# GpSimd's two-operand work in the mixers goes to VectorE, its scalings to ScalarE, and two expert splits move behind the selection

## The chip, the core and the metric

The kernel runs on one core of a Trainium2 chip. The core has five instruction queues that run side by side, each in the order in which its instructions stand: TensorE for matrix products (PE, with its weight loads as PEld), VectorE (DVE), ScalarE (ACT), GpSimd (POOL) and SyncE (SP), which issues the transfers. They wait for each other by semaphores. The metric is the time of one execution on the device in microseconds (us).

## The reference

Two layers over 256 latent tokens and 256 context tokens, 1024 channels wide. Each layer is a mixer of three branches and then a channel mixer: a dense SwiGLU in layer 0, and eight experts, of which each token takes two, in layer 1.

```python
def token_mixer(h, hc, ...):                 # one layer's mixer, cut
    zp, zr, zq, zk, zv, zg = jnp.split(h @ w_in, splits, axis=-1)      # 1024 -> 5,344
    ...                                                                # context tokens alike
    wkv, wkv_c = bidirectional_wkv(lat, cx, need_ctx_out)              # a recurrence, both ways
    nat = neighbourhood_attention(q, k, ...)
    branches = (pool_branch(zp, pool_w, pool_scale),                   # mean over a window - identity
                rwkv_readout(wkv, lat, bonus_rk, gn_g, gn_b, gate_g2), nat)
    y = gated_merge(branches, zg, w_branch, w_out)                     # sum of sigmoid(gate) * proj

# the recurrence, for each head a 64 x 64 state S:
#   S = S * w_t - (S kk_t) kka_t^T + v_t k_t^T ;  o_t = S r_t
# the last part: out = sum over experts e of gate[e] * swiglu(h, w1[e], w3[e], w2[e])
```

## The kernel before

Everything is float32. A product is made of three: each operand is split into a rounded part `hi` and the rest `lo`, and TensorE adds hi·hi, hi·lo and lo·hi (lines L491 to L493, L246 to L248 and L1845 to L1847 are these three for different places). A weight tile of 128x1024 comes in by a transfer (`wraw`), ScalarE rounds it (`whi`, L204) and a second engine subtracts (`wlo`, L208, in `split`). Which engine does that, `wload` counts: in the mixers every other tile and the first two are GpSimd's, the rest VectorE's. In the dense layer every other tile is GpSimd's too, and in the experts none.

A mixer has these stages, and TensorE's order in them is written by lanes with fixed costs (class `Order`), so that products of the input projection fill the time in which a chain of the recurrence waits:

- the front (85 to 265 us in mixer 0, 1200 to 1320 us in mixer 1): the input projection tile by tile, a shift between tokens (`s`, L523, L525 and L527 take the product out of PSUM), and for each of four channel groups and two directions the recurrence's operands (`operands`, L630 to L651) and the pooled branch (`z`, L1206 to L1210);
- the attention, with the triangular solve of the recurrence beside it (`solve`, L791 to L832), to 436 us and 1490 us;
- the core (436 to 655 us and 1490 to 1610 us): eight rounds n over chunks of 64 tokens, both directions d in each round. `reads` multiplies the state's rows with `Ga` (L928) and copies `Y` out (L931); `products` makes the next chunk's matrices, for chunks that need an output in the `sm` banks (L871; L882 and L877 take them out), else in `ch` banks (L891, L882); `solved` (L939, L942) and `state` (L951, L960, L962) end the round. There are two `sm` banks, so the second direction's L871 begins when the first's L882 and L877 have emptied them;
- readout, merge and output projection.

In the core the other half of `Ga` comes from memory. `chunk` sends for it and scales it, for two heads of each direction:

```python
            for hh, p, q in self.HEADS:
                a = e["Ga"][q, hh]
                nc.sync.dma_start(a, src[p, :, 64:128])
                nc.gpsimd.tensor_tensor(a, a, g[q].to_broadcast([64, 4, 64]), op=OP.mult)
```

The transfer (L861) can start when L928 has read the `Ga` before it. The order of VectorE's instructions is made by a scheduler from the program; it is not written out.

Of the kernel before, what the change touches and what calls it, by code (L numbers as in the profile page):

```python
# [103 lines left out]
class Builder:  # L104
    def __init__(self, ctx, tc, I, out, dbg=None):
        self.ctx, self.tc, self.nc, self.I, self.out = ctx, tc, tc.nc, I, out
        self.dbg = dbg or {}
        self.nlo, self.lo_first = 0, 0
        self.pre, self.ahead = [], []
        self.raws, self.parted, self.pin = (), (), False  # L110
        self.nraw = self.nparts = 0
        self.banks = {}
        self.norm_banks = ExitStack()
        self.sq = self.rs = None
        self.hw = 512
        self.cpool = ctx.enter_context(tc.tile_pool(name="consts", bufs=1))
        self.dram = ctx.enter_context(tc.tile_pool(name="dr", bufs=1, space=DRAM))
        nc = self.nc
        cst = self.cpool.tile([128, C_N], F32, name="cst")
        nc.sync.dma_start(cst, I["cst"])  # L120
        self.cst = cst
        self.ident = cst[:, C_ID:C_ID + 128]
        self.mask = cst[:, C_MSK:C_MSK + 128]
        self.i2 = cst[:, C_I2:C_I2 + 64]
        self.ob = cst[:, C_OB:C_OB + 128]
        self.ones = cst[:, C_ON:C_ON + 128]
        self.tiny = ctx.enter_context(tc.tile_pool(name="tiny", bufs=6))
        hb = self.cpool.tile([40, 4, 128], F32R, name="hb")
        with tc.tile_pool(name="hb0", bufs=1) as hp:
            hb0 = hp.tile([40, 4, 128], F32, name="hb0")  # L130
            nc.sync.dma_start(hb0, I["heads"])
            nc.vector.tensor_copy(hb, hb0)
        self.hb = hb
        self.vec = []
        for l in range(2):
            v = self.cpool.tile([128, V_N], F32, name=f"vec{l}")
            nc.sync.dma_start(v, I["vec"][l])
            self.vec.append(v)
        self.mod = [[None] * 6 for _ in range(2)]
# [61 lines left out]
    def split(self, hi, lo, src, hi_eng="act", lo_eng="dve"):  # L201
        nc = self.nc
        if hi_eng == "act":
            nc.scalar.copy(hi, src)  # L204
        else:
            nc.vector.tensor_copy(hi, src)
        e = nc.gpsimd if lo_eng == "pool" else nc.vector
        e.tensor_tensor(lo, src, hi.bitcast(F32), op=OP.subtract)  # L208

    def wload(self, src, n, lo_eng=None, hi_eng="act"):  # L210
# [20 lines left out]
        for s, raw in raws:  # L231
            self.split(hi[:, s], lo[:, s], raw[:, :s.stop - s.start], hi_eng, lo_eng)
# [318 lines left out]
    def rwkv_front(self, l, full, order):  # L551
# [20 lines left out]
        self.split(lwh, lwl, lw, "act", "pool")  # L572
# [27 lines left out]
        def glo_tile():  # L600
            glo = yield from self.shifted_out(l, 1, T_GLO, full, self.u)
            nc.scalar.activation(glo[0:96, :], glo[0:96, :], AF.Tanh, scale=0.5)
            nc.gpsimd.tensor_scalar(glo[0:96, :], glo[0:96, :], 0.5, 0.5, op0=OP.mult, op1=OP.add)
            self.glo = glo
# [17 lines left out]
        def operands(c, d):  # L622
# [25 lines left out]
            nc.gpsimd.tensor_copy(st[:, :, 1, 0].rearrange("p (s n) -> p s n", s=2), o4(kk)[:, :, :, 0])  # L648
            nc.scalar.copy(s4(4), o4(vc))
            nc.gpsimd.tensor_tensor(s4(0), n4(G), o4(rc), op=OP.mult)  # L650
            nc.gpsimd.tensor_tensor(self.order(kd, 0), self.order(kd, 0), self.order(rc, d), op=OP.mult)  # L651
# [94 lines left out]
    def out_gates(self, l, n, order):  # L746
# [4 lines left out]
        for c in range(4):  # L751
# [6 lines left out]
            nc.scalar.copy(gate, gp)  # L758
            nc.gpsimd.tensor_scalar(bo, bo, v[:, V_GNB + c:V_GNB + c + 1], None, op0=OP.add)
            nc.gpsimd.tensor_tensor(bo, bo, gate, op=OP.mult)  # L760
            nc.sync.dma_start(self.bonus[c], bo)
            nc.gpsimd.tensor_scalar(gate, gate, v[:, V_GNG + c:V_GNG + c + 1], None, op0=OP.mult)
# [76 lines left out]
    def chunk(self, d, n, need_o):  # L839
# [17 lines left out]
        if n:  # L857
            g = self.gq[d][:, :, n - 1].unsqueeze(2)
            for hh, p, q in self.HEADS:
                a = e["Ga"][q, hh]  # L860
                nc.sync.dma_start(a, src[p, :, 64:128])  # L861
                nc.gpsimd.tensor_tensor(a, a, g[q].to_broadcast([64, 4, 64]), op=OP.mult)
# [82 lines left out]
    def state(self, e, new, d, n):  # L945
# [15 lines left out]
        for hh, p, q in self.HEADS:  # L961
            nc.gpsimd.tensor_tensor(nS[q], new["XV"][q, hh], g[q].to_broadcast([64, 4, 64]), op=OP.mult)  # L962
# [72 lines left out]
    def readout(self, l, n, pool):  # L1035
# [13 lines left out]
        for c in range(4):  # L1049
# [4 lines left out]
            nc.gpsimd.tensor_tensor(ga[c], ga[c], w, op=OP.mult)  # L1054
# [127 lines left out]
    def pool_branch(self, l, full, order):  # L1182
# [6 lines left out]
        def pool_tile(g):  # L1189
# [10 lines left out]
            for i, z in enumerate(zs):  # L1200
# [3 lines left out]
                while w < win:  # L1204
                    nxt = self.pb.tile([128, 272], F32, name="z", tag="z")
                    nc.gpsimd.tensor_tensor(nxt[:, :m - w], cur[:, :m - w], cur[:, w:m], op=OP.add)  # L1206
                    cur, m, w = nxt, m - w, 2 * w
                ti = t[:, 256 * i:256 * i + 256]
                nc.gpsimd.tensor_tensor(ti, cur[:, 8 - h:264 - h], iv, op=OP.mult)
                nc.gpsimd.tensor_tensor(ti, ti, z[:, 8:264], op=OP.subtract)  # L1210
# [12 lines left out]
    def branch_split(self, tiles, n, mixed=False):  # L1223
        res = []
        for t in tiles:
            hi = self.u2(n, F32R)
            lo = self.u2(n, F32R)
            self.split(hi, lo, t, "act", "dve" if mixed and len(res) % 2 == 0 else "pool")
# [3 lines left out]
    def merge_branch(self, l, b, br, f, full, gate, acc):  # L1232
# [10 lines left out]
        nc.gpsimd.tensor_tensor(acc, acc, gate, op=OP.add)  # L1243
# [10 lines left out]
    def merge_steps(self, l, b, br, f, full, gate, acc):  # L1254
# [9 lines left out]
        if acc is not None:  # L1264
            nc.gpsimd.tensor_tensor(acc, acc, gate, op=OP.add)

    def mixer(self, l, x, full, xnew, done=lambda: None):
# [13 lines left out]
        self.lo_mod, self.lo_pool, self.lo_first = 2, 1, 2  # L1281
# [116 lines left out]
        def early_gate(f):  # L1398
            g = lambda n: self.gp.tile([128, n], F32, name="gp", tag="gp")
            self.gate[f] = yield from self.gate_steps(l, 1, f, full, g, "pool")  # L1400
# [77 lines left out]
        br = self.branch_split(self.wkv, n, True)  # L1478
# [176 lines left out]
    def moe(self, l, x):  # L1655
        nc, tc, I = self.nc, self.tc, self.I
        ident = self.ident
        with ExitStack() as ex:
# [21 lines left out]
            with P2("scrm2", 3) as self.sp, tc.high_priority(100000):  # L1680
# [41 lines left out]
                sel = self.selected(0, pos, msk, two, keep)  # L1722
# [404 lines left out]
```

## Time and profile before

| | |
|---|---|
| device time, median of 3 runs | 2495.73 us (2491.53 to 2501.99) |
| the profiled execution | 2494.59 us |
| its span in the trace | 2492.8 us, 40223 instructions |
| its mean granted TensorE clock | 0.961 |
| busy in the span: PE, DVE | 2318.3 us (93%), 1809.5 us (73%) |
| busy in the span: ACT, POOL | 1276.6 us (51%), 576.6 us (23%) |

Times of the trace count from the start of the span. The profiled execution's own time is 1.8 us above its span, and 1.1 us below the median of the runs. The granted clock is a share of full speed: 0.50 in a stretch means 1.2 instead of 2.4 GHz.

### The profile page before, as it was taken

The page shows a single profiled execution, that of the slowest core. Times are in us where ns is not written, and L with a number is a line of the kernel's source. Part 1 is how long each engine was busy: PE and PEld are TensorE (multiplying, and loading weights), DVE is VectorE, ACT ScalarE, POOL GpSimd, SP SyncE. Part 2 cuts the span into 40 slices and gives each one's busy share as a digit, 9 for nine tenths or more (in the row PEclk, how much of TensorE's full clock was granted, in tenths as well). Part 3 has the DMA queues.
Part 4 walks back from the last instruction along what each step waited for, and adds up shares of the span by engine and source line. Part 5 has one row for each costly group of instructions (what it writes and reads, how often), then busy time and mean ns, then how long its engine had stood idle before and what let it go on. Part 6 is the DMA issues. An engine that isn't in the chain of part 4 may idle for free. (4 is left out here: it accounts for less than half of the span.)

```text
span 2492.8 us, 40223 instructions
## 1 busy us (share of the span) xinstructions
PE 2318.3 (93%) x15206; PEld 1858.1 (75%) x15206; DVE 1809.5 (73%) x2723; ACT 1276.6 (51%) x1864; POOL 576.6 (23%) x487
## 2 busy tenths in 40 slices
PE   6899999988899999999779889979999999999998
PEld 4567667777678888777566678768888888888876
DVE  3784667656677656875785755568999999989997
ACT  3553554222243222234554444347777777777775
POOL 1255421243351221122553335430000000000000
PEclk8999998999899999999989989989999999999999
DMA  6364233554433444772473326675999999999995
GB/s 250 95 168 132 77 98 93 173 151 154 144 118 104 150 144 144 235 241 78 128 186 97 116 89 198 194 262 177 367 351 339 360 363 336 343 361 344 356 343 194
DMA packets 224141, 514.33 MB, mean 206 GB/s; under 512 B 70490, under 2 KB 104666, under 8 KB 222786
## 3 DMA queue, kind: packets, MB, share of 16 engines
q1 hardware_dynamic: 223938, 511.67, 61.1%
q8 instruction: 122, 2.00, 0.3%
q14 instruction: 81, 0.66, 0.1%
HBM read 484.79 MB, written 26.74 MB: 205 GB/s over the span
## 5 line engine op out<-in xcount | busy, mean ns | idle before, releaser
L204 ACT CAST whi<-wraw 128x1024 fp32r<-128x1024 f32 (+2 forms) x753 | 754.3, 1019 | 615.9 <-DMA wraw<-in_ffn 178.9
L208 DVE TENSOR_TENSOR wlo<-wraw,whi 128x1024 fp32r<-128x1024 f32 (+2 forms) x629 | 756.4, 1232 | 137.3 <-ACT whi L204 126.5
L208 POOL TENSOR_TENSOR wlo<-wraw,whi 128x1024 fp32r<-128x1024 f32 (+2 forms) x124 | 263.9, 2129 | 722.3 <-ACT whi L204 714.6
L491 PE MATMUL mm<-h,whi 128*128 128x512 f32 (+1 forms) x864 | 347.7, 402 | 33.3 <-DVE s L527 13.6
L493 PE MATMUL mm<-h,wlo 128*128 128x512 f32 (+1 forms) x864 | 321.4, 372 | 11.9 <-DVE wlo L208 6.2
L492 PE MATMUL mm<-h,whi 128*128 128x512 f32 (+1 forms) x864 | 322.0, 373 | 5.5 <-DVE h L476 5.4
L1845 PE MATMUL mm<-whi,xh 128*128 128x512 f32 (+1 forms) x768 | 289.2, 377 | 0.0
L1846 PE MATMUL mm<-whi,xl 128*128 128x512 f32 (+1 forms) x768 | 288.1, 375 | 0.0
L1847 PE MATMUL mm<-wlo,xh 128*128 128x512 f32 (+1 forms) x768 | 281.5, 376 | 1.3 <-DVE wlo L208 1.3
L491 PEld LDWEIGHTS mm<-h,whi 128*128 128x128 f32 x864 | 172.4, 200 | 86.2 <-issue 36.1
L493 PEld LDWEIGHTS mm<-h,wlo 128*128 128x128 f32 x864 | 172.2, 199 | 42.7 <-DVE wlo L208 8.5
L492 PEld LDWEIGHTS mm<-h,whi 128*128 128x128 f32 x864 | 172.9, 200 | 33.5 <-DVE h L476 9.2
L247 PE MATMUL mm<-h,whi 128*128 128x512 f32 (+1 forms) x448 | 170.6, 382 | 2.6 <-DVE h L208 2.6
L248 PE MATMUL mm<-h,wlo 128*128 128x512 f32 (+1 forms) x448 | 170.8, 382 | 0.4 <-POOL wlo L208 0.3
L246 PE MATMUL mm<-h,whi 128*128 128x512 f32 (+1 forms) x448 | 169.8, 380 | 0.0
L1847 PEld LDWEIGHTS mm<-wlo,xh 128*128 128x128 f32 x768 | 144.1, 188 | 29.2 <-DVE wlo L208 2.1
L1846 PEld LDWEIGHTS mm<-whi,xl 128*128 128x128 f32 x768 | 144.4, 188 | 27.0
L1845 PEld LDWEIGHTS mm<-whi,xh 128*128 128x128 f32 x768 | 144.6, 188 | 26.5
L1874 PE MATMUL mm<-wlo,hh 128*128 128x512 f32 x352 | 139.6, 397 | 0.8 <-DVE wlo L208 0.8
L1873 PE MATMUL mm<-whi,hl 128*128 128x512 f32 x352 | 139.1, 395 | 0.0
L1872 PE MATMUL mm<-whi,hh 128*128 128x512 f32 x352 | 138.7, 394 | 0.0
L368 DVE SCALAR_TENSOR_TENSOR scr<-wraw,cb 128x512 f32<-128x512 f32 x96 | 75.7, 806 | 57.6 <-DMA wraw<-in_w_mod 57.0
(378 smaller groups left out, 4024.4 us busy)
## 6 DMA issues: line engine op xcount, KB each, us to landing
wraw<-in_moe SPq DMA_DIRECT2D x516, 512.0 KB, 5.5
wraw<-in_w_in SPq DMA_DIRECT2D x108, 512.0 KB, 3.7
wraw<-in_w_mod SPq DMA_DIRECT2D x96, 512.0 KB, 4.6
wraw<-in_ffn SPq DMA_DIRECT2D x60, 512.0 KB, 3.9
rakbv<-std SPq DMA_DIRECT2D x32, 640.0 KB, 5.3
wraw<-in_w_branch SPq DMA_DIRECT2D x48, 256.0 KB, 2.7
std<-st SPq DMA_DIRECT2D x16, 640.0 KB, 5.0
wraw<-in_w_out SPq DMA_DIRECT2D x13, 512.0 KB, 4.1
```

The source lines that it names most:

```text
L204: nc.scalar.copy(hi, src)
L208: e.tensor_tensor(lo, src, hi.bitcast(F32), op=OP.subtract)
L246: nc.tensor.matmul(ps, wh, xh, start=i == 0, stop=False)
L247: nc.tensor.matmul(ps, wh, xl, start=False, stop=False)
L248: nc.tensor.matmul(ps, wl, xh, start=False, stop=i == n - 1)
L491: nc.tensor.matmul(ps, wh, xh, start=i == 0, stop=False)
L492: nc.tensor.matmul(ps, wh, xl, start=False, stop=False)
L493: nc.tensor.matmul(ps, wl, xh, start=False, stop=i == n - 1)
L1845: nc.tensor.matmul(ps, xh[:, k0 + k], hi[:, w], start=k0 + k == 0, stop=False)
L1846: nc.tensor.matmul(ps, xl[:, k0 + k], hi[:, w], start=False, stop=False)
L1847: nc.tensor.matmul(ps, xh[:, k0 + k], lo[:, w], start=False, stop=k0 + k == 7)
L1874: nc.tensor.matmul(y, hid[k][0], lo[:, w], start=False, stop=k == KF - 1)
```

## The change

In the two mixers GpSimd keeps its memsets and nothing else. The splits of weights, of the branches and of the small `lw`, the products and sums of the operands (L650, L651), of the pooled branch (L1206, L1209, L1210), of `Ga` and `S` (L862, L962), of the readout (L1054) and of the merges (L1243, L1265) are VectorE's; two scalings and a small copy (L603, L762, L648) are ScalarE's, and two steps of the gate (L759, L760) become one VectorE instruction that reads PSUM. The dense layer's splits stay as they were. In the experts, the splits of the third and fourth weight tile get an ordering edge behind the selection matrices `sel` of the routing. VectorE's queue grows from 3297 to 3656 instructions, ScalarE's from 2493 to 2511, and GpSimd's falls from 496 to 103.

```diff
@@ split, wload
-        e.tensor_tensor(lo, src, hi.bitcast(F32), op=OP.subtract)
+        return e.tensor_tensor(lo, src, hi.bitcast(F32), op=OP.subtract)
...
-            self.split(hi[:, s], lo[:, s], raw[:, :s.stop - s.start], hi_eng, lo_eng)
+            ins = self.split(hi[:, s], lo[:, s], raw[:, :s.stop - s.start], hi_eng, lo_eng)
+            if self.nlo in self.late_lo:
+                self.behind(ins)
@@ front
-        self.split(lwh, lwl, lw, "act", "pool")
+        self.split(lwh, lwl, lw, "act", "dve")
-            nc.gpsimd.tensor_scalar(glo[0:96, :], glo[0:96, :], 0.5, 0.5, op0=OP.mult, op1=OP.add)
+            nc.scalar.activation(glo[0:96, :], glo[0:96, :], AF.Identity, scale=0.5, bias=half[0:96])
-            nc.gpsimd.tensor_copy(st[:, :, 1, 0].rearrange("p (s n) -> p s n", s=2), o4(kk)[:, :, :, 0])
+            nc.scalar.copy(st[:, :, 1, 0].rearrange("p (s n) -> p s n", s=2), o4(kk)[:, :, :, 0])
-            nc.gpsimd.tensor_tensor(s4(0), n4(G), o4(rc), op=OP.mult)
-            nc.gpsimd.tensor_tensor(self.order(kd, 0), self.order(kd, 0), self.order(rc, d), op=OP.mult)
+            nc.vector.tensor_tensor(s4(0), n4(G), o4(rc), op=OP.mult)
+            nc.vector.tensor_tensor(self.order(kd, 0), self.order(kd, 0), self.order(rc, d), op=OP.mult)
@@ gate of the readout
-            nc.scalar.copy(gate, gp)
-            nc.gpsimd.tensor_scalar(bo, bo, v[:, V_GNB + c:V_GNB + c + 1], None, op0=OP.add)
-            nc.gpsimd.tensor_tensor(bo, bo, gate, op=OP.mult)
+            nc.vector.scalar_tensor_tensor(bo, bo, v[:, V_GNB + c:V_GNB + c + 1], gp, op0=OP.add, op1=OP.mult)
-            nc.gpsimd.tensor_scalar(gate, gate, v[:, V_GNG + c:V_GNG + c + 1], None, op0=OP.mult)
+            nc.scalar.activation(gate, gp, AF.Copy, scale=v[:, V_GNG + c:V_GNG + c + 1])
@@ chunk, state, readout
-                nc.gpsimd.tensor_tensor(a, a, g[q].to_broadcast([64, 4, 64]), op=OP.mult)
+                nc.vector.tensor_tensor(a, a, g[q].to_broadcast([64, 4, 64]), op=OP.mult)
-            nc.gpsimd.tensor_tensor(nS[q], new["XV"][q, hh], g[q].to_broadcast([64, 4, 64]), op=OP.mult)
+            nc.vector.tensor_tensor(nS[q], new["XV"][q, hh], g[q].to_broadcast([64, 4, 64]), op=OP.mult)
-            nc.gpsimd.tensor_tensor(ga[c], ga[c], w, op=OP.mult)
+            nc.vector.tensor_tensor(ga[c], ga[c], w, op=OP.mult)
@@ pooled branch (three lines alike), merges (two alike), branch_split
-                    nc.gpsimd.tensor_tensor(nxt[:, :m - w], cur[:, :m - w], cur[:, w:m], op=OP.add)
+                    nc.vector.tensor_tensor(nxt[:, :m - w], cur[:, :m - w], cur[:, w:m], op=OP.add)
-            nc.gpsimd.tensor_tensor(acc, acc, gate, op=OP.add)
+            nc.vector.tensor_tensor(acc, acc, gate, op=OP.add)
-            self.split(hi, lo, t, "act", "dve" if mixed and len(res) % 2 == 0 else "pool")
+            self.split(hi, lo, t, "act", "dve")
@@ mixer, moe
-        self.lo_mod, self.lo_pool, self.lo_first = 2, 1, 2
+        self.lo_mod, self.lo_pool, self.lo_first = 2, 0, 0
-                sel = self.selected(0, pos, msk, two, keep)
+                sel = self.selected(0, pos, msk, two, lambda ins: setattr(self, "mark", keep(ins)))
+
+                self.late_lo = (3, 4)
```

The changed program's lines stand one to three further down than here; the rows below show each program's own. First VectorE's queue in the core of mixer 1, in the fifth of the eight rounds (it begins at 1561.8 us in the trace of before). `Y`, `Ga` and `Gr` are the copies and matrices named above, `gq` holds the scalings of one direction. Before:

```order
L931 COPY Y<-ch 128x256 x2
L882 TENSOR_TENSOR Ga<-sm,cst 64x256
L877 TENSOR_TENSOR Gr<-sm,cst 128x256
L882 TENSOR_TENSOR Ga<-sm,cst 64x256
L877 TENSOR_TENSOR Gr<-sm,cst 128x256
L942 COPY XV<-ch 64x256
```

and of the change:

```order
L932 COPY Y<-ch 128x256 x2
L863 TENSOR_TENSOR Ga<-Ga,gq_13337 64x256 x2
L863 TENSOR_TENSOR Ga<-Ga,gq_13338 64x256
L883 TENSOR_TENSOR Ga<-sm,cst 64x256
L878 TENSOR_TENSOR Gr<-sm,cst 128x256
L883 TENSOR_TENSOR Ga<-sm,cst 64x256
L878 TENSOR_TENSOR Gr<-sm,cst 128x256
L863 TENSOR_TENSOR Ga<-Ga,gq_13338 64x256
L943 COPY XV<-ch 64x256
L209 TENSOR_TENSOR wlo<-wraw,whi 128x1024
```

The scalings of `Ga`, which wait for their transfers, stand ahead of the instructions that empty the `sm` banks. Second, VectorE's queue in the front of mixer 0 (at 172 to 179 us in the trace of before), up to the instruction that takes a product of the projection out of PSUM. Before:

```order
L638 TENSOR_TENSOR s_1372<-s_1372,kz 128x512
L663 TENSOR_TENSOR V_687<-ch,cst 128x512
L643 TENSOR_TENSOR st<-s_1372,s_1367 128x8x64
L644 SCALAR_TENSOR_TENSOR s_1367<-s_1364,s_1367 128x512
L525 SCALAR_TENSOR_TENSOR s_1428<-mm,vec_73,s_1428 128x2x255
L645 SCALAR_TENSOR_TENSOR st<-s_1367,kz 128x8x64
L527 SCALAR_TENSOR_TENSOR s_1428<-mm,vec_73,s_1428 128x2x255
```

and of the change:

```order
L653 TENSOR_TENSOR st<-s_1362,s_1099 128x8x64
L666 TENSOR_TENSOR V_687<-ch,cst 128x512
L209 TENSOR_TENSOR wlo<-wraw,whi 128x1024
L641 TENSOR_TENSOR s_1372<-s_1372,kz 128x512
L528 SCALAR_TENSOR_TENSOR s_1428<-mm,vec_73,s_1428 128x2x255
L646 TENSOR_TENSOR st<-s_1372,s_1367 128x8x64
L530 SCALAR_TENSOR_TENSOR s_1428<-mm,vec_73,s_1428 128x2x255
```

A split and a product that were GpSimd's stand in the queue, and L527 (now L530) has moved ahead of L644 and L645 (now L647 and L648). Third, the routing: the rows around the splits, before:

```order
L208 TENSOR_TENSOR wlo<-wraw,whi 128x1024
L264 SCALAR_TENSOR_TENSOR rs<-rs 128x2
L208 TENSOR_TENSOR wlo<-wraw,whi 128x1024
L262 SCALAR_TENSOR_TENSOR rs<-rs 128x2
```

and of the change, there and at the place where the two splits now stand:

```order
L267 SCALAR_TENSOR_TENSOR rs<-rs 128x2
L209 TENSOR_TENSOR wlo<-wraw,whi 128x1024
L265 SCALAR_TENSOR_TENSOR rs<-rs 128x2
...
L1735 TENSOR_TENSOR gate<-gate,nm 128x16
L209 TENSOR_TENSOR wlo<-wraw,whi 128x1024 x2
L1745 TENSOR_REDUCE most<-sm 128x1
L1817 SCALAR_TENSOR_TENSOR xl<-sm,mod_3_9278,xh 128x256
```

One split is left in the chain of `rs`, on which the experts' choice rests, and two stand behind the selection, ahead of the first operand `xl` of the experts.

## Rows read from the trace of the kernel before

**Rows 1.** Page, part 1: engine, busy us (share of span), instructions.

```profile
PE 2318.3 (93%) x15206; PEld 1858.1 (75%) x15206; DVE 1809.5 (73%) x2723; ACT 1276.6 (51%) x1864; POOL 576.6 (23%) x487
```

**Rows 2.** Windows: start:end and length, busy time of PE, PEld, DVE, ACT, POOL, PEclk, DMA.

```profile
85.00:265.00 180.00, 164.33 (x889) 117.03 (x888) 113.01 (x144) 85.22 (x136) 89.56 (x87) 0.95 0.50 130
...
1200.00:1320.00 120.00, 93.84 (x690) 72.94 (x690) 96.67 (x109) 68.88 (x118) 70.29 (x62) 0.88 0.63 163
...
1490.00:1610.00 120.00, 116.04 (x1937) 104.91 (x1937) 63.20 (x134) 46.96 (x98) 60.81 (x75) 1.00 0.61 179
```

**Rows 3.** Timeline, front of mixer 0: start, duration, engine, line, tiles; brackets: idle before.

```profile
173.10 2.39 POOL L208 TENSOR_TENSOR wlo<-wraw,whi 128x1024 fp32r<-128x1024 f32 x1 [1.46 <-ACT whi L204]
...
173.32 2.72 DVE L643 TENSOR_TENSOR st<-s,s 128x512 f32<-128x512 f32 x1
...
178.36 0.73 DVE L527 SCALAR_TENSOR_TENSOR s<-mm,vec,s 128x510 f32<-128x510 f32 x1
...
179.24 0.54 PE L491 MATMUL mm<-h,whi 128*128 128x512 f32 x1 [4.24 <-DVE s L527]
```

**Rows 4.** Timeline, front of mixer 0, another place.

```profile
197.55 2.36 POOL L208 TENSOR_TENSOR wlo<-wraw,whi 128x1024 fp32r<-128x1024 f32 x1
...
197.82 2.63 DVE L643 TENSOR_TENSOR st<-s,s 128x512 f32<-128x512 f32 x1 [2.46 <-ACT s L634]
...
199.96 0.79 PE L493 MATMUL mm<-h,wlo 128*128 128x512 f32 x1 [2.84 <-POOL wlo L208]
```

**Rows 5.** Timeline, core of mixer 0.

```profile
446.87 2.39 POOL L208 TENSOR_TENSOR wlo<-wraw,whi 128x1024 fp32r<-128x1024 f32 x1 [25.36 <-ACT whi L204]
...
447.43 2.37 DVE L368 SCALAR_TENSOR_TENSOR scr<-wraw,cb 128x512 f32<-128x512 f32 x1 [6.57 <-DMA wraw<-in_w_mod]
...
449.85 0.69 DVE L368 SCALAR_TENSOR_TENSOR scr<-wraw,cb 128x512 f32<-128x512 f32 x1
```

**Rows 6.** Timeline, front and solve of mixer 1.

```profile
1284.15 1.96 DVE L646 TENSOR_TENSOR st<-s,kz 128x504 f32<-128x504 f32 x1 [0.82 <-ACT s L632]
...
1302.84 0.60 DVE L264 SCALAR_TENSOR_TENSOR rs<-rs 128x16 f32<-128x16 f32 x1
...
1316.76 0.80 PE L1215 MATMUL sm<-scr 128*128 128x256 f32 x1 [2.67 <-POOL scr L1210]
```

**Rows 7.** Windows: one half-clock stretch; columns as in group 2.

```profile
1316.10:1323.00 6.90, 6.24 (x15) 4.96 (x16) 6.86 (x6) 3.10 (x6) 4.44 (x6) 0.51 0.27 96
```

**Rows 8.** Timeline, attention of both mixers.

```profile
390.13 0.21 DVE L803 TENSOR_TENSOR svT<-svT,svt 128x31 f32<-128x31 f32 x1
...
1447.23 0.58 PE L493 MATMUL mm<-h,wlo 128*128 128x256 f32 x1 [1.75 <-POOL wlo L208]
...
1457.36 2.40 DVE L803 TENSOR_TENSOR svT<-svT,svt 128x31 f32<-128x31 f32 x1
...
1464.31 0.66 PE L1162 MATMUL ch<-cst,pr 128*128 128x128 f32 x4 [3.25 <-ACT pr L1156]
```

**Rows 9.** Timeline, routing of the experts.

```profile
1678.99 1.22 DVE L208 TENSOR_TENSOR wlo<-wraw,whi 128x1024 fp32r<-128x1024 f32 x1
...
1683.49 0.60 PE L1708 MATMUL nx<-msk,rc 128*128 128x8 f32 x2 [6.09 <-DVE msk L1706]
```

**Rows 10.** Timeline, core of mixer 1, one round.

```profile
1561.80 3.36 SPq L861 DMA_DIRECT2D Ga<-std  x4
...
1561.81 0.94 DVE L931 COPY Y<-ch 128x256 f32<-128x256 f32 x2 [0.32 <-PE ch L928]
...
1564.71 0.42 DVE L882 TENSOR_TENSOR Ga<-sm,cst 64x256 f32<-64x256 f32 x1 [1.97 <-PE sm L871]
...
1566.54 1.16 PE L871 MATMUL sm<-rakbv 64*128 64x128 f32 x16
...
1566.76 2.71 POOL L862 TENSOR_TENSOR Ga<-Ga,gq 64x256 f32<-64x256 f32 x4 [4.33 <-DMA Ga<-std]
```

**Rows 11.** One line's summary (L861): DMAs that load Ga.

```profile
DMA to landing us min/median/max: 2.3/4.0/7.1
```

More of the change, by code (lines that the diff above doesn't have):

```diff
@@ L110, in __init__ @@
         self.raws, self.parted, self.pin = (), (), False
+        self.late_lo = ()
         self.nraw = self.nparts = 0
@@ L1205, in pool_tile @@
                     nxt = self.pb.tile([128, 272], F32, name="z", tag="z")
-                    nc.gpsimd.tensor_tensor(nxt[:, :m - w], cur[:, :m - w], cur[:, w:m], op=OP.add)
+                    nc.vector.tensor_tensor(nxt[:, :m - w], cur[:, :m - w], cur[:, w:m], op=OP.add)
                     cur, m, w = nxt, m - w, 2 * w
                 ti = t[:, 256 * i:256 * i + 256]
-                nc.gpsimd.tensor_tensor(ti, cur[:, 8 - h:264 - h], iv, op=OP.mult)
-                nc.gpsimd.tensor_tensor(ti, ti, z[:, 8:264], op=OP.subtract)
+                nc.vector.tensor_tensor(ti, cur[:, 8 - h:264 - h], iv, op=OP.mult)
+                nc.vector.tensor_tensor(ti, ti, z[:, 8:264], op=OP.subtract)
             order.add(2, mixed(g, t), self.waits[5] * ns * (g + 4))
@@ L1221, in pool_branch, with branch_split @@
         return [(lambda: True, pool_tile(g)) for g in range(4)]
-    def branch_split(self, tiles, n, mixed=False):
+    def branch_split(self, tiles, n):
         res = []
@@ L1264, in merge_steps @@
         if acc is not None:
-            nc.gpsimd.tensor_tensor(acc, acc, gate, op=OP.add)
+            nc.vector.tensor_tensor(acc, acc, gate, op=OP.add)
     def mixer(self, l, x, full, xnew, done=lambda: None):
@@ L1399, in early_gate @@
             g = lambda n: self.gp.tile([128, n], F32, name="gp", tag="gp")
-            self.gate[f] = yield from self.gate_steps(l, 1, f, full, g, "pool")
+            self.gate[f] = yield from self.gate_steps(l, 1, f, full, g)
         def dense():
@@ L1477, in mixer @@
             self.dump(f"pool{c}", self.pool[c])
-        br = self.branch_split(self.wkv, n, True)
+        br = self.branch_split(self.wkv, n)
         m = []
```

## The prediction

> **What bounds the kernel now.** I read the page's first part first: TensorE is busy in 93% of the span, VectorE in 73%, GpSimd in 23% [rows 1]. So a change to VectorE and GpSimd can pay only where TensorE waits, and the windows by stage tell where that is. The experts leave TensorE 792.0 − 780.2 us of idle in the trace, and GpSimd does nothing there; the room lies in the mixers. In the front of mixer 0 TensorE is busy for 164.3 of 180 us, in the front of mixer 1 for 93.8 of 120, in the core of mixer 1 for 116.0 of 120, that is with 4.0 us to spare [rows 2]. A wait costs more than itself, since the granted clock falls behind it: after the 2.67 us that ended at 1316.76 [rows 6] the next stretch of 6.9 us went at 0.51 [rows 7], so that some 3.4 us more were lost.
>
> Then I looked, for each wait of TensorE in the mixers, at who ended it and what stood ahead of that on its engine. Few are ended by GpSimd itself: 2.84 us at 199.96, 1.75 us at 1447.23, 2.67 us at 1316.76 [rows 4, 6, 8]. More are ended by VectorE, and there the trace shows a thing that matters for this change: a VectorE instruction with both inputs in SBUF that runs beside a GpSimd one ends when that ends. L643 took 2.63 us beside a split of GpSimd's [rows 4] and 2.72 us in another place [rows 3], the same form L368 2.37 us beside a split and 0.69 us behind it [rows 5], and an L803 of 31 columns took 2.40 us [rows 8].
>
> **What the change removes and adds.** Two costs go: those stretched instructions, and GpSimd's own length (2.36 us for a split that takes VectorE 1.22 us, [rows 4, 9]). One comes: 359 more instructions in VectorE's queue, one behind the other, with their waits. In the front of mixer 1 VectorE is busy for 96.7 of 120 us already, and GpSimd's 70.3 us there [rows 2] come over at about half, by the two lengths of a split. So I price it place by place, at VectorE's undisturbed lengths: 0.69 us for 128x512 with two inputs [rows 5], 0.42 us for 64x256 [rows 10], 1.22 us for a split of 128x1024 [rows 9].
>
> *Front of mixer 0, at 179.* Before, L643 begins at 173.32, is held to 2.72 us, and L527, for which TensorE waits, ends at 179.09 [rows 3]. In the new order a split comes first; its `whi` is there at 173.10, when GpSimd began it. Then 1.22 + 0.69 + 0.73 + 0.69 + 0.73 us (split, L638, L525, L643, L527 by before's lines) end at 177.16: −1.9 us. Bounds: 0 if the inputs come later, −4.2, the whole wait. *At 200*, GpSimd's split ends at 199.91 and lets TensorE go. VectorE was free at 197.55 (it had waited for 2.46 us until 197.82, [rows 4]); from there 1.22 us end 1.1 us earlier: −1.1, bounds 0 and −2.8.
>
> *Core of mixer 0.* The stretched L368 gives back 2.37 − 0.69 = 1.7 us [rows 5], and the new order puts splits and scalings of `Ga` between, ahead of the instructions that empty `sm`, as in the other core below. But in these rounds VectorE waits for weights anyway (6.57 us ahead of that L368), which covers most of it. I take 0, between −4 (two such places given back) and +5 (two stalls as below).
>
> *Front of mixer 1.* From 1284.15 to 1303.44, 19.3 us [rows 6], VectorE works through 26 instructions; at the lengths that their forms have undisturbed they would take 12.7 us. The new order has 40 there: two splits, five of 0.69 us and seven of 0.42 us more, 8.8 us. 12.7 + 8.8 = 21.5, so +2.2 us. The wait at 1316.76 ends with GpSimd's last step of the pooled branch, which VectorE does in less; I give it 1.2 of its 2.67 us: together +1.0, bounds −2.7 and +3.5.
>
> *Attention of mixer 1.* L803's 2.40 us stood on the way to the softmax whose product waits 3.25 us at 1464.31; another of that size took 0.21 us, so −2.2. The split at 1447.23 gains half of its length against a full queue: −1.0 of the 1.75 [rows 8]. Together −3.2, bounds −5.0 and 0.
>
> *Routing.* Two splits of 1.22 us stand in the chain of `rs` ahead of the choice of experts, on which TensorE waits for 6.09 us [rows 9]. One stays, so −1.2; both then stand ahead of `xl`, so bounds −1.2 and 0.
>
> *Core of mixer 1.* Here a wait is added. Scaling `Ga` waits for a transfer that is sent when L928 has read the last one; on GpSimd that stopped nothing that the round needs at once. In VectorE's queue three scalings now stand ahead of L882 and L877. In the round at 1561.8 VectorE is done with `Y` at 1562.75, GpSimd began on `Ga` at 1566.76 after 4.33 us of waiting [rows 10], and a transfer takes 2.3 to 7.1 us from issue to landing [rows 11]. So VectorE waits until 1566.76, scales for 3 × 0.42 us, and empties the first `sm` bank with two more of 0.42, by 1568.86. The other direction's L871 began at 1566.54 and needs that bank: 2.3 us later. What is queued behind (L942, a split, L960) shifts with it. Four rounds have this shape, 9.2 us; the three before them have L942 behind the scalings, and I give them 2.8 us together, between 0 and 2.3 each. Of these 12 us TensorE's idle of 4.0 us in this stage can take up a part: +8, bounds 0 and 16.
>
> ScalarE's new work (16 small copies, two scalings) lies beside its idle half; TensorE nowhere waits for it, and I give it nothing, at most 2 us. The same holds for the merges, where TensorE waits little: 0, within 2 us either way. The dense layer's splits don't move.
>
> Sum: −1.9 − 1.1 + 0 + 1.0 − 3.2 − 1.2 + 8 = +1.6 us. On the profiled execution's 2494.59 us (its span of 2492.8 and 1.8 us around it) that is 2496.2. The median of the runs, 2495.73, is 1.1 us above that execution, less than the runs differ; I predict **2496 us**, no change.
>
> **A rule weighed.** That the two engines hold each other up is shown by [rows 3, 4, 5, 8], at 2.4 to 2.7 us for what takes 0.69 or less. The Trainium skill, SBUF — State Buffer, "Who interferes with whom", says why: VectorE's second read port is GpSimd's, and who issues first holds it alone. The trace agrees, by those rows. Read with Perfetto Trace Analysis, "Optimizing GPSIMD Operations", which prefers other engines, it would make the move a plain gain; that is the first rival. By the order alone it is not one.
>
> **The rivals.** *Faster: the freed port shows everywhere.* For it: the stretched instructions are found in every stage of the mixers, and the waits that they make are followed by half-clock stretches. If the places above come near their lower bounds (−4.2 − 2.8 − 4 − 2.7 − 5.0 − 1.2 = −19.9), the core of mixer 1 costs 5 us because the transfers land earlier in a calmer round, and two stretches like that of [rows 7] go (−6.8), the sum is −21.7: 2473 us. Against it: VectorE's load rises in every stage, and in the front of mixer 1 by more than it is freed.
>
> *Slower: VectorE stands behind `Ga`.* Place: the core of mixer 1, and the two rounds of mixer 0. The price: nothing of the 12 us is taken up, each of the four stalls of 2.3 us brings a half-clock stretch (the 2.67 us wait cost 3.4 us; I take half, 1.7 each, 6.8), the core of mixer 0 costs 5 us, and the other terms, −6.4 together, stay: −6.4 + 12 + 6.8 + 5 = +17.4: 2512 us. For it: the landing rows. It decides once `Ga` lands more than about 1 us behind `Y`. Against it: TensorE has other products in these rounds.
>
> *The change hardly acts*: where VectorE has taken a job it does it as late as GpSimd did. That gives the time of before and falls in with my forecast.
>
> **How the numbers follow.** No change (my forecast, with 2486 to 2506 as its own range) 0.40; the freed port 0.34; VectorE behind `Ga` 0.26. A difference of 0.5%, some 12.5 us, is about what a measurement of this kernel can tell from no change. The first rival's 2473 and the second's 2512 lie beyond it, but parts of both fall within: faster 0.34, same 0.42, slower 0.24. The range for 8 in 10 reaches to both rivals and a little past them: 2470 to 2515 us.
>
> **What would show it.** Right: L643 and L368 at 0.69 us everywhere in the mixers; TensorE's wait at 179 near 2.3 us and that at 200 near 1.7; VectorE waiting for the transfer of `Ga` in the core of mixer 1 for some 4 us a round, and TensorE waiting for L871; that stage some 8 us longer, the attention and front of mixer 0 some 3 us shorter each. Wrong: the core of mixer 1 as long as before (then `Ga` lands in time and the kernel is faster), or VectorE's waits on other transfers in the fronts, which I did not count.

## The result, and the profile after the change

The changed kernel takes 2467.16 us (median of 4 runs, 2457.90 to 2469.23), the kernel before 2496.47 us beside it (2491.53 to 2501.99). The ratio is 0.9875, with an interval of 0.9853 to 0.9897: 1.25% faster, below the range of 2470 to 2515 us. The profiled execution took 2465.34 us, with a span of 2463.4. Times below are medians of all of a kernel's runs; one run, of `idle_core`, took 2833.24 us at a granted clock of 0.741, where the others of that kernel had 0.963 to 0.973, and is left out of its ratio.

The page's first part, to be read against [rows 1]:

```profile
PE 2313.5 (94%) x15206; PEld 1853.6 (75%) x15206; DVE 1895.2 (77%) x3082; ACT 1281.3 (52%) x1882; POOL 95.5 (4%) x94
```

GpSimd gave up 481 us of work, and VectorE is busy for only 86 us more. In the code of the changed kernel the same statements stand one to three lines lower: L862, L871, L877, L882, L931 and L643 of before are L863, L872, L878, L883, L932 and L646; the transfer L861 is L862.

To see where the time came from, I took the start of the same TensorE instruction in both traces, stage by stage. The stages are those of the prediction, in before's times:

| stage (before's us) | predicted, us | measured, us |
|---|---|---|
| front of mixer 0 (85 to 265) | -3.0 | -15.3 |
| attention and solve of mixer 0 (to 430) | 0 | -2.5 |
| core of mixer 0 (to 655) | 0 (-4 to +5) | -17.7 |
| readout and merge of mixer 0 (to 735) | 0 (within 2) | +11.0 |
| dense layer (to 1200) | 0 | +1.4 |
| front of mixer 1 (to 1320) | +1.0 (-2.7 to +3.5) | -11.9 |
| attention of mixer 1 (to 1490) | -3.2 (-5.0 to 0) | -4.7 |
| core of mixer 1 (to 1610) | +8 (0 to 16) | +17.2 |
| readout, merge, routing (to 1690) | -1.2 | -6.4 |
| experts | 0 | -0.5 |
| sum | +1.6 | -29.4 |

A stage of one trace has a spread, and a bound set one instruction further on moves a step by up to 1 us or so. Four of the kernels below (`idle_gpsimd`, `idle_memset`, `no_late_split`, `ga_four_buffers`) have VectorE's instructions of mixer 0 in the same order as the changed kernel. By the same method their core of mixer 0 is 12.0 to 13.7 us shorter than before, and their readout and merge 2.2 to 4.0 us longer. So about 4 of the 17.7 us and 7 of the 11.0 belong to this one execution. The core of mixer 1 is 12.6 to 17.9 us longer in the three of them that leave it as it is in the change.

The windows of the changed kernel's trace over the two fronts and the two cores show how (columns as in [rows 2]; the bounds are moved by the shifts of the table, so that the same work lies inside):

```profile
85.00:250.00 165.00, 156.82 (x890) 112.23 (x889) 120.23 (x207) 85.91 (x144) 1.96 (x16) 1.00 0.53 142
417.00:620.00 203.00, 189.92 (x2245) 150.37 (x2238) 158.61 (x359) 53.00 (x102) 0.00 (x0) 0.98 0.55 167
1177.00:1285.00 108.00, 88.76 (x684) 69.60 (x682) 92.44 (x149) 65.82 (x120) 2.65 (x12) 0.92 0.69 176
1450.00:1587.00 137.00, 125.42 (x1942) 112.97 (x1941) 94.14 (x209) 46.86 (x96) 0.00 (x0) 0.94 0.52 156
```

In the front of mixer 0 TensorE's idle went from 180 - 164.3 = 15.7 to 165 - 156.8 = 8.2 us, and its busy time, for the same matmuls, from 164.3 to 156.8 at a granted clock of 1.00 instead of 0.95. So the 15 us are 7.5 us of waits and 7.5 us of clock. In the front of mixer 1, by the same reckoning, 6.9 us are waits and 5.1 clock. For the core of mixer 0 this is the window before:

```profile
436.00:655.00 219.00, 195.88 (x2208) 155.39 (x2208) 134.53 (x284) 51.44 (x99) 75.53 (x73) 0.94 0.50 152
```

Idle went from 23.1 to 13.1 us there and busy time from 195.9 to 189.9: 10.0 us of waits and 6.0 of clock, of the 16.0 us that these two windows differ by. In the core of mixer 1 it is the other way round: idle from 4.0 to 11.6 us, busy from 116.0 to 125.4, the clock from 1.00 to 0.94. That is +7.6 for waits and +9.4 for the clock behind them.

The stretched instructions are gone. The summaries of two lines in the trace of before (minimum, median and longest duration in ns):

```profile
L643 DVE TENSOR_TENSOR st<-s,s x16: 676/687/2719, 113.2 to 1299.8; 128x512 f32<-128x512 f32 x16
...
L368 DVE SCALAR_TENSOR_TENSOR scr<-wraw,cb x96: 674/684/2891, 409.9 to 1007.2; 128x512 f32<-128x512 f32 x96
```

and of the same two in the changed kernel:

```profile
L646 DVE TENSOR_TENSOR st<-s,s x16: 679/684/697, 112.1 to 1267.3; 128x512 f32<-128x512 f32 x16
...
L371 DVE SCALAR_TENSOR_TENSOR scr<-wraw,cb x96: 674/684/695, 394.5 to 984.2; 128x512 f32<-128x512 f32 x96
```

What came in is a wait of VectorE. One round of the core of mixer 1 in the changed kernel's timeline, to be read against [rows 10]:

```profile
1528.49 3.46 SPq L862 DMA_DIRECT2D Ga<-std  x4
...
1529.01 0.74 DVE L932 COPY Y<-ch 128x256 f32<-128x256 f32 x2
...
1532.17 1.39 DVE L863 TENSOR_TENSOR Ga<-Ga,gq 64x256 f32<-64x256 f32 x3 [2.41 <-DMA Ga<-std]
...
1533.57 0.42 DVE L883 TENSOR_TENSOR Ga<-sm,cst 64x256 f32<-64x256 f32 x1
...
1534.41 0.46 PE L872 MATMUL sm<-rakbv 64*128 64x128 f32 x2 [1.16 <-issue]
...
1535.36 0.95 PE L872 MATMUL sm<-rakbv 64*128 64x128 f32 x10 [0.49 <-DVE Gr L878]
```

VectorE is done with `Y` at 1529.75, stands for 2.41 us before the transfer of `Ga`, and only then empties the `sm` banks that the second direction's L872 needs. The list of waits over the whole trace (what waits, for whom, us in total, times, longest) gives for these two:

```profile
DVE Ga L863 <- DMA Ga<-std: 11.6, 8, 3.3
```

```profile
PE sm L872 <- DVE Gr L878: 5.6, 9, 0.9
```

Before, the second was

```profile
PE sm L871 <- DVE Gr L877: 0.7, 3, 0.3
```

A new wait that I had not looked for stands in the readout of mixer 0, here in the timeline of the changed kernel:

```profile
618.53 0.69 DVE L371 SCALAR_TENSOR_TENSOR scr<-wraw,cb 128x512 f32<-128x512 f32 x1 [4.17 <-DMA wraw<-in_w_mod]
...
621.50 0.42 DVE L987 TENSOR_TENSOR wk<-wk,ch 128x256 f32<-128x256 f32 x1
...
621.97 2.07 PE L1049 MATMUL nx<-wk,cst 128*128 128x512 f32 x2 [2.78 <-DVE wk L987]
```

VectorE waits 4.17 us for a weight transfer and has three longer instructions behind it, one of them (a merge sum, L1266) former GpSimd work; the small L987, for which TensorE waits, comes last. By the table's method 7.2 of the 11.0 us are lost at this place. With VectorE's instructions in the same order TensorE waits here for 3.1 us in `idle_gpsimd`, 1.7 in `idle_memset`, and not at all in `no_late_split` and `ga_four_buffers`, where VectorE waits for its weights for 3.1 us in the second and 0.6 and 0.5 in the last two; so TensorE's wait hangs on when the transfer lands. Last, the routing, against the 6.09 us of [rows 9]:

```profile
1655.04 0.60 PE L1709 MATMUL nx<-msk,rc 128*128 128x8 f32 x2 [2.47 <-DVE msk L1707]
```

### The profile page after: what moved, and what is told of

Its sections match the earlier page's. It is cut to its first block, busy times and chain, and to the rows that moved or that the text cites. A ratio compares the mean times of both kernels' runs of the same rounds, so it can differ in the third digit from the quotient of the medians.

```text
span 2463.4 us, 39956 instructions
## 1 busy us (share of the span) xinstructions
PE 2313.5 (94%) x15206; PEld 1853.6 (75%) x15206; DVE 1895.2 (77%) x3082; ACT 1281.3 (52%) x1882; POOL 95.5 (4%) x94
## 5 line engine op out<-in xcount | busy, mean ns | idle before, releaser
L209 DVE TENSOR_TENSOR wlo<-wraw,whi 128x1024 fp32r<-128x1024 f32 (+1 forms) x719 | 838.8, 1193 | 156.2 <-ACT whi L205 144.8
L494 PE MATMUL mm<-h,whi 128*128 128x512 f32 (+1 forms) x864 | 341.4, 395 | 24.1 <-ACT u L1080 6.2
L495 PE MATMUL mm<-h,whi 128*128 128x512 f32 (+1 forms) x864 | 315.2, 365 | 5.3 <-DVE h L479 5.3
L494 PEld LDWEIGHTS mm<-h,whi 128*128 128x128 f32 x864 | 168.4, 195 | 75.6 <-issue 25.0
L495 PEld LDWEIGHTS mm<-h,whi 128*128 128x128 f32 x864 | 169.1, 196 | 31.5 <-DVE h L479 8.3
L249 PE MATMUL mm<-h,whi 128*128 128x512 f32 (+1 forms) x448 | 172.3, 386 | 1.2 <-ACT whi L205 1.2
L250 PE MATMUL mm<-h,whi 128*128 128x512 f32 (+1 forms) x448 | 170.7, 382 | 0.0
L373 DVE SCALAR_TENSOR_TENSOR wraw<-wraw,cb 128x1024 f32<-128x1024 f32 x80 | 102.2, 1283 | 11.9 <-DMA wraw<-in_w_mod 10.4
L209 POOL TENSOR_TENSOR wlo<-wraw,whi 128x1024 fp32r<-128x1024 f32 (+1 forms) x34 | 79.5, 2340 | 764.3 <-DMA wraw<-in_ffn 428.4
```

Of the source, the lines that this page charges most:

```text
L209: return e.tensor_tensor(lo, src, hi.bitcast(F32), op=OP.subtract)
L249: nc.tensor.matmul(ps, wh, xh, start=i == 0, stop=False)
L250: nc.tensor.matmul(ps, wh, xl, start=False, stop=False)
L494: nc.tensor.matmul(ps, wh, xh, start=i == 0, stop=False)
L495: nc.tensor.matmul(ps, wh, xl, start=False, stop=False)
```

## The experiments

The theory after the result had two parts: the gain comes from GpSimd no longer reading SBUF beside VectorE, and some 17 us of it are lost again because VectorE stands behind the transfers of `Ga`. The rivals: the gain comes from something else in the change (a faster engine for the splits, another order, the late splits); and the core of mixer 1 is longer because VectorE is fuller there, or because of `S`.

**The port.** `idle_gpsimd` is the changed kernel with 98 subtractions on GpSimd whose result nobody reads, in the two fronts.

```diff
@@ wload, only while a front runs
+                for k in range(s.start, s.stop, 512):
+                    h = hi[:, k:k + 512].bitcast(F32)
+                    self.nc.gpsimd.tensor_tensor(self.idle, h, h, op=OP.subtract)
```

> The changed kernel with work for GpSimd added that nobody waits for: in the two fronts, behind each split of a weight tile, GpSimd subtracts that tile's rounded half from itself into a tile that is never read, 98 instructions of 128x512. TensorE's, VectorE's, ScalarE's and SyncE's queues stand exactly as in the change. Theory, the shared access to SBUF held VectorE up before the change: L646 and its like are stretched to 1 to 2.5 us again, the front of mixer 0 grows from 165 us to 170 to 178, that of mixer 1 from 111 to 114 to 118, the whole takes 2474 to 2485 us. Rival, only GpSimd's own length and the new order of VectorE's queue made the gain: nothing is stretched, both fronts stay within 2 us, the whole within 4 us of 2467.

Measured: 2504.12 us (ratio to before 1.0001, 0.9978 to 1.0024). As much as the whole gain is lost, more than expected. The front of mixer 0 lasts 22 us longer than in the changed kernel, that of mixer 1, counted from 1120 us on, 17. The change had gained 15.3 and 11.9 us there, and the core of mixer 0 keeps its gain (13.7 us). So the run shows what GpSimd's reading can cost, and not that all of the gain came from it. `idle_memset` replaces each subtraction:

```diff
-                    self.nc.gpsimd.tensor_tensor(self.idle, h, h, op=OP.subtract)
+                    self.nc.gpsimd.tensor_copy(self.idle[:, :1], h[:, :1])
+                    for _ in range(3):
+                        self.nc.gpsimd.memset(self.idle, 0.0)
```

> As the run with idle GpSimd work in the fronts (2504 us), but GpSimd only writes: each subtraction of 128x512 is a copy of one column of the rounded half and three memsets of 128x512 behind it, so that GpSimd is busy at the same places for about as long. The other queues stand as in the change. Theory, VectorE is held up by GpSimd's reading of SBUF beside its own second input: next to nothing is stretched, the whole stays within 6 us of the change's 2467. Rival, any GpSimd work beside VectorE's holds it up: the fronts grow as with the subtractions, the whole takes 2490 us or more.

Measured: 2463.02 us (0.9859, 0.9838 to 0.9881), as the changed kernel. The groups of VectorE's instructions in 85 to 265 us (count | busy, mean ns | idle before) show one and the same form, the split of 128x1024, in four kernels. Before:

```profile
L208 DVE TENSOR_TENSOR wlo<-wraw,whi 128x1024 fp32r<-128x1024 f32 x11 | 16.4, 1494 | 14.4 <-ACT whi L204 14.4
```

The changed kernel:

```profile
L209 DVE TENSOR_TENSOR wlo<-wraw,whi 128x1024 fp32r<-128x1024 f32 x23 | 28.0, 1220 | 19.5 <-ACT whi L205 19.4
```

With idle subtractions on GpSimd:

```profile
L210 DVE TENSOR_TENSOR wlo<-wraw,whi 128x1024 fp32r<-128x1024 f32 x20 | 30.0, 1499 | 20.4 <-ACT whi L206 20.4
```

With idle memsets:

```profile
L210 DVE TENSOR_TENSOR wlo<-wraw,whi 128x1024 fp32r<-128x1024 f32 x23 | 28.0, 1220 | 19.9 <-ACT whi L206 19.9
```

The mean goes 1494, 1220, 1499, 1220 ns. And the windows over the front of mixer 0, with the subtractions (bounds moved by that kernel's own shift)

```profile
87.00:273.00 186.00, 170.59 (x887) 120.39 (x887) 136.28 (x207) 86.12 (x144) 66.96 (x56) 0.91 0.49 126
```

and with the memsets

```profile
85.00:250.00 165.00, 155.40 (x884) 110.94 (x883) 118.75 (x206) 84.85 (x145) 94.61 (x176) 1.00 0.54 143
```

GpSimd busy for 94.6 us costs nothing where it writes and reads no more than single columns, and busy for 67.0 us it costs 21 us where it reads whole tiles: 7 us of waits and 14 of clock. The Trainium skill, SBUF — State Buffer, "Who interferes with whom", says just this of a VectorE instruction with two inputs in SBUF: it contends with a GpSimd instruction that reads SBUF, not with one that only writes it. The trace agrees, by these four rows.

`idle_core` puts such subtractions, in pieces of 128x128, into the cores (276 more instructions of GpSimd).

> The changed kernel with work for GpSimd that nobody waits for in the cores of both mixers: behind each split of a weight tile there, GpSimd subtracts the tile's rounded half from itself, in pieces of 128x128, into a tile that is never read. Theory, as in the fronts: the core of mixer 0 (203 us in the change, 219 before) gets back 5 to 16 us by stretched instructions, the whole takes 2474 to 2485 us. Rival, in the core the gain came from GpSimd's length (S, and the merges' sums): the stage stays within 3 us, the whole within 5 of 2467.

Measured: 2473.97 us (0.9900, 0.9874 to 0.9926). In the trace the core of mixer 0 is 6.5 us shorter than before, against 12.0 to 13.7 us in the four kernels that leave it as it is in the change, so that at least 5.5 us come back. The mean split on VectorE took 1523 ns in this stage before, 1222 in the change and 1309 here: some of the stretch is back. That speaks for the port; as times this kernel and the changed one are not told apart.

`only_splits_on_vector` is the kernel before with nothing but the mixers' splits of weights moved:

```diff
-        self.lo_mod, self.lo_pool, self.lo_first = 2, 1, 2
+        self.lo_mod, self.lo_pool, self.lo_first = 2, 0, 0
```

> The kernel before with only the mixers' weight splits moved to VectorE (87 instructions, GpSimd's longest); the operands, the pooled branch, Ga, S and the merges stay GpSimd's. Theory: these splits are about half of GpSimd's time in the mixers and so of what it holds up: the fronts and the core of mixer 0 are together 12 to 25 us shorter, the whole takes 2475 to 2488 us. Rival: VectorE's queue only grows, 2497 us or more.

Measured: 2481.93 us (0.9929, 0.9910 to 0.9948), about half of the gain. In the profiled run the front of mixer 0 is only 3.6 us shorter, and the mean split on VectorE still takes 1425 ns there: the operands, which are still GpSimd's, go on holding VectorE up. The two fronts and the core of mixer 0 are together some 12.6 us shorter, at the lower end of what was expected.

**The transfer of `Ga`.** `ga_on_gpsimd` is the changed kernel with one line put back.

```diff
-                nc.vector.tensor_tensor(a, a, g[q].to_broadcast([64, 4, 64]), op=OP.mult)
+                nc.gpsimd.tensor_tensor(a, a, g[q].to_broadcast([64, 4, 64]), op=OP.mult)
```

> The changed kernel with one line taken back: the scaling of Ga is GpSimd's again (56 instructions), all else as in the change. Theory, VectorE's queue stands behind a transfer: the core of mixer 1, 137 us long in the change and 120 before, falls to 120 to 125 us, TensorE's waits for L872 there go, and the whole takes 2450 to 2456 us (2467 in the change). Rival, the core is longer because VectorE has more to do there (94 us busy instead of 63): only 56 x 0.42 = 24 us of that load go in both cores, the stage stays above 130 us and the whole above 2460 us.

Measured: 2449.28 us (0.9804, 0.9782 to 0.9825). The core of mixer 1 takes as long as before (0.9 us less from 1490 to 1610). `only_ga_on_vector` is the other half: the kernel before with that one line moved.

> The kernel before with one line of the change: the scaling of Ga is VectorE's, all else is GpSimd's as before. Theory, VectorE's queue stands behind a transfer: the core of mixer 1 grows from 120 us to 130 to 138, the whole takes 2505 to 2515 us. Rival, it is the load of all the moved work together: the core of mixer 1 grows by less than 5 us, the whole takes 2496 to 2501 us.

Measured: 2532.32 us (1.0126, 1.0105 to 1.0148), 32 us slower, which is more than expected; the core of mixer 1 is 22.8 us longer, that of mixer 0 8.3. In its trace the front of mixer 1, where no scaling of `Ga` stands, is some 8 us longer too, for which I have no reason. The line's summary shows both costs in one kernel, the longest at 2636 ns beside GpSimd's reading, and the waits:

```profile
L862 DVE TENSOR_TENSOR Ga<-Ga,gq x56: 406/422/2636, 459.1 to 1634.8; 64x256 f32<-64x256 f32 x56
...
  DMA Ga<-std: 17.2, 12
```

`ga_s_on_gpsimd` puts L963, the scaling of `S`, back as well.

> The version with Ga on GpSimd (2449 us) and the scaling of S (56 instructions) back on GpSimd too. It waits for no transfer, only for VectorE's L961. Theory: taking it from GpSimd was no loss, since there it holds VectorE's splits up: 2449 to 2458 us. Rival: in the cores each instruction less in VectorE's queue counts, 2440 to 2446 us.

Measured: 2447.87 us (0.9796, 0.9777 to 0.9814), no different from `ga_on_gpsimd`: `S` waits for no transfer, and where it is scaled does not matter.

`ga_four_buffers` keeps the scalings on VectorE and gives `Ga` four buffers in mixer 1, so that the transfer may go a round earlier.

```diff
-        for k, bufs in (("Ga", 2), ("XV", 4)):
+        for k, bufs in (("Ga", 4 if self.tok0 else 2), ("XV", 4)):
```

> The changed kernel, Ga scaled on VectorE as in the change, with four Ga tiles instead of two in the core of mixer 1 (mixer 0 as in the change), so that a round's transfer need not wait until L929 has read the last one. VectorE's queue in the core stands as in the change. Theory, VectorE waits there for the transfer and TensorE for VectorE: with the transfers a round earlier the wait goes, the core of mixer 1 falls from 137 us to 118 to 124, the whole takes 2450 to 2456 us. Rival, it is VectorE's load: the stage stays at 132 us or more, the whole above 2460.

Measured: 2468.31 us (0.9898, 0.9862 to 0.9933): a miss. Its trace says why. From the timeline of this kernel, ahead of the first round's `Y`:

```profile
1455.38 2.56 SPq L862 DMA_DIRECT2D Ga<-std  x4
...
1461.88 0.42 DVE L863 TENSOR_TENSOR Ga<-Ga,gq 64x256 f32<-64x256 f32 x1 [2.78 <-DMA Ga<-std]
1463.27 1.31 DVE L863 TENSOR_TENSOR Ga<-Ga,gq 64x256 f32<-64x256 f32 x3
```

All seven groups of transfers did go one round earlier (the last at 1544.49 instead of 1564.77 us), but the scheduler moved the scalings with them, right behind their transfers. VectorE waits for them 13.5 us in 8 times, in the changed kernel 11.6. So VectorE's queue did not stand as in the change, which the expectation had taken for granted. The core of mixer 1 takes 132 us in this trace, no less than in `idle_memset` with the order of the change (132.5), so that this run alone could not tell the place in the queue from VectorE's load. `ga_four_buffers_dense` adds the dense layer's splits on VectorE to this.

> The last but one with the dense layer's splits on VectorE too, so that in the layers GpSimd has memsets alone. If both gains add, 2440 to 2448 us, the level of the version with Ga on GpSimd and those splits on VectorE (2439 us); if the freed access to SBUF in the cores counts beside it, 2432 to 2439 us.

Measured: 2456.19 us (0.9845, 0.9811 to 0.9878), a miss too. So the last run leaves the buffers and the engine as they are and moves only the place in the queue. `ga_scaled_late`:

```diff
-                nc.vector.tensor_tensor(a, a, g[q].to_broadcast([64, 4, 64]), op=OP.mult)
@@ scaled, called ahead of state in each round; self.xv is the last L943 of the round
+            ins = self.nc.vector.tensor_tensor(a, a, g[q].to_broadcast([64, 4, 64]), op=OP.mult)
+            self.tc.add_manual_dep(ins.ins, self.xv.ins.name, ..., reason="order")
```

> The changed kernel, with the scalings of Ga still on VectorE, but ordered behind the second L943 of the round instead of right behind their transfers. Nothing else is changed by hand; the rows of VectorE around them move with it. Theory (VectorE in its order stands behind the transfer; the engine itself is not the trouble): the waits of L863 for the transfer of Ga, 11.6 us in the changed kernel, all but go, and the core of mixer 1 comes out 10 to 17 us shorter, as it did with the scalings on GpSimd: 2450 to 2458 us. Rival (VectorE's added load in the core, 56 instructions of 0.42 us, is the price, wherever they stand): 2463 to 2470 us, as the changed kernel. In a third case the scalings, now near the end of the round, hold L960 up: the waits move there, and the time is 2463 or more with TensorE waiting for L928 or L951.

Measured: 2447.82 us (0.9814, 0.9789 to 0.9839), as with the scalings on GpSimd. The summary of the line (now L867) names no wait at all; the windows over the core of mixer 1, from 1440 us on:

```profile
1440.00:1564.00 124.00, 120.69 (x1973) 109.57 (x1968) 96.14 (x210) 48.34 (x100) 0.00 (x0) 0.99 0.58 174
```

By the same matmuls, before's stretch of 120 us (1490 to 1610) takes 120 here, within 1 us, with VectorE's whole new load in it. So neither the engine nor its load costs anything that can be seen in this stage; the place behind the transfer cost the 17 us (12.6 to 17.9 in the traces with the order of the change).

**The rest of the change.** `no_late_split` leaves the two expert splits where they were.

```diff
-                self.late_lo = (3, 4)
```

> The changed kernel without the ordering edge of the two expert splits; the mixers as in the change. Theory, two splits of 1.22 us in the chain of the routing: TensorE's wait for the choice of experts is 1 to 2 us longer, the whole 2468 to 2470 us. Rival, the edge gives the time back ahead of the experts' first operand: the stretch from the routing to the experts' first products is as long as in the change, within 0.5 us.

Measured: 2474.33 us (0.9896, 0.9879 to 0.9912). The interval overlaps that of the changed kernel; in the trace the step at the routing is 1.8 us longer, so the edge does gain there, and what the whole gains by it is not told from nothing.

`ga_gpsimd_dense_vector` goes further: `Ga` on GpSimd, and the dense layer's splits on VectorE too.

```diff
@@ dense layer
-            self.lo_mod, self.lo_pool, self.lo_first = 2, 1, 0
+            self.lo_mod, self.lo_pool, self.lo_first = 2, 0, 0
```

> The version with Ga on GpSimd (2449 us) and the dense layer's splits, 34 of them GpSimd's in every version so far, on VectorE too. Theory: in the dense layer VectorE's instructions with two SBUF inputs are no longer stretched and TensorE's waits for GpSimd's splits (1.7 us at the largest) go; but TensorE is busy there for 342 of 349 us, so at most 7 us come: 2442 to 2447 us. Rival: VectorE's 34 more splits of 1.2 us come late for TensorE instead, 2449 us or more.

Measured: 2439.39 us (0.9768, 0.9748 to 0.9789), the best of all kernels here. The windows over the dense layer, first in the changed kernel, where TensorE waited five times for a split of GpSimd's (6.8 us):

```profile
768.00:1117.00 349.00, 342.21 (x1469) 274.93 (x1467) 224.89 (x328) 93.23 (x123) 74.92 (x39) 1.00 0.53 175
```

and here, where it doesn't wait:

```profile
768.00:1110.00 342.00, 342.00 (x1478) 276.86 (x1477) 210.90 (x370) 94.80 (x126) 3.99 (x14) 1.00 0.55 177
```

VectorE does more instructions there in less time, 210.9 instead of 224.9 us.

## Why the prediction was wrong

The forecast of no change was wrong; the first rival, "the freed port shows everywhere" at 2473 us, had the sign and the cause, and came out 6 us short of the gain. That it came so near is in part luck: it gave the two fronts and the core of mixer 0 together -13.7 us, and -6.8 for the clock (measured -44.9 in all), and the core of mixer 1 +5 (measured +17.2).

*What it read rightly.* That a two-input VectorE instruction beside GpSimd is stretched ([rows 3, 4, 5, 8]) and that this ends: L643 and L368 are at 0.69 to 0.70 us throughout, and the runs with idle work show that GpSimd's reading does this. One word was off: such an instruction doesn't end when GpSimd's does. In [rows 3, 4, 5] it ends 0.54 to 0.55 us after it (the split at 173.10 ends at 175.49, L643 at 176.04), most of the 0.69 us that it takes undisturbed: it was held up, and then ran. That VectorE would stand behind `Ga`, and L871 behind VectorE: shown by the rows of the round and by `ga_on_gpsimd`, `only_ga_on_vector` and `ga_scaled_late`. That the late split is worth about 1.2 us at the routing (1.8 in the trace). That ScalarE's new work is hidden (52% busy, 51% before).

*The step that failed: "I price it place by place".* The fronts and the core of mixer 0 were priced at the waits that I had picked out, -3.0, +1.0 and 0; they measured -15.3, -11.9 and -17.7. Two things were left out of each term. The first is the rest of the chain: in the front of mixer 0 the waits of 4.24 and 2.84 us [rows 3, 4] both went whole, where I had given back 1.9 and 1.1. These two alone make 7.1 us, and all waits of the stage together fell by 7.5, so the places were the right ones, and the price of each was too low. I had begun each sum at a time of the trace before (`whi` there at 173.10, VectorE free at 197.55) and so left in what had been held up ahead of it, while the mean split on VectorE was 1494 ns and not 1220 in the whole stage. That this made the difference is argued from the means and not tested place by place. The second of the two waits ended with a split of GpSimd's own, and no run parts what GpSimd's length cost there from what the port cost. The other thing left out is the clock. The text said that "a wait costs more than itself", from [rows 7], and then put that into the rivals alone. In the front of mixer 0 half of the gain is clock (7.5 of 15.0 us), in that of mixer 1 5.1 of 12, in the core of mixer 0 6.0 of 16. For the core of mixer 0 only a part is tested: of the 12.0 to 13.7 us that four kernels gain there, at least 5.5 come back in `idle_core`; the rest is open.

*The term that was mis-sized: the core of mixer 1.* Predicted +8, bounds 0 to 16, measured +17.2. The waits were sized well, though VectorE stands for less than I put down for a round (11.6 us in all, 3.3 at the longest): TensorE's idle there grew by 7.6 us. The 9.4 us of clock behind them were missing. The second rival had them, at 6.8 us.

*The step that counted queue length as a cost.* "By the order alone it is not one" (a plain gain): for the front of mixer 1, 8.8 us of added instructions were set against 6.6 us of stretch to make +2.2. But VectorE had slack there (96.7 of 120 us busy before, 92.4 of 108 after), and a longer queue delays only what stands behind; in the front this is argued, and in the core of mixer 1 `ga_scaled_late` shows it. The readout of mixer 0, to which I gave 0 within 2 us, came out at +11.0, of which 7.2 are lost behind a transfer of weights; kernels with the same order lose 2.2 to 4.0 us in that stage, so it is not the length of the queue that the 7.2 us show. What those 2.2 to 4.0 us are, and why the merge of mixer 1 gained, was not isolated. Perfetto Trace Analysis, "Optimizing GPSIMD Operations", in the Trainium skill, prefers other engines where possible. The runs agree for the change as a whole (1.25% faster) and for the weight splits moved alone (0.7%); for `S` it made no difference, and for `Ga`, which cost time, `ga_scaled_late` shows that it was the place and not the engine.

## What to carry to other kernels

Look for two-input VectorE instructions that are longer than their own form elsewhere: if GpSimd reads beside them, price the whole chain at the undisturbed lengths, and count for each wait that goes the half-clock stretch behind it as well. When an instruction that waits for a transfer changes engines, look at what stands behind it in the new queue; if it can't stay on an idle engine, order it behind the work that doesn't need the transfer, since with more buffers alone the scheduler brought both forward together here. And before a step of a few us in one trace is explained, look at the same step in other kernels that leave that stage as it is.

## What the runs showed of the chip

The clock's share was larger than expected. In the front of mixer 0 a kernel with 15.4 us of TensorE idle in 186 us had a granted clock of 0.91 (`idle_gpsimd`), one with 15.7 in 180 us 0.95 (before), one with 8.2 in 165 us 1.00 (after): by these three the sum of the idle alone does not set it. The second surprise is on GpSimd's side: one of the idle subtractions of 128x512 took 1.03 us at the least and 4.84 at the most, by spans that are rough for this engine.
